# A planner that lets VectorE and GpSimd take turns and deals elementwise work to either

## The chip, the core and the metric

The kernel runs on one core of a Trainium2 chip. A core has five engines, each with its own queue of instructions that it works off in order: TensorE (PE, matrix products), VectorE (DVE), ScalarE (ACT), GpSimd (POOL) and SyncE (SP, which here issues the transfers). The metric is the device time of one execution in microseconds (us). Three runs of the kernel before gave 2014.33, 2015.26 and 2022.29 us; the median is 2015.26 us.

## What is computed

One layer of a hybrid decoder on 16 meta tokens and 1024 tokens of 1024 features, all in float32. The part that the change touches is the mixer's input:

```python
h = xn @ w_in                      # xn: (1040, 1024), w_in: (1024, 8192)
b_c, c_c, h_c, q, k, v, g_conv, g_attn = jnp.split(h, list(splits), axis=-1)
y_conv = b_c * causal_dwconv(c_c * h_c, conv_w_mix)
o = stick_breaking_attention(q.reshape(hd), k.reshape(hd), v.reshape(hd))
gate_conv = jax.nn.sigmoid(g_conv + b_gate[0])
gate_attn = jax.nn.sigmoid(g_attn + b_gate[1])
merged = gate_conv * (y_conv @ w_proj_conv) + gate_attn * (o @ w_proj_attn)
return merged @ w_out
```

Attention weighs the earlier position s for the position t by sigmoid(z_ts) times the product of (1 - sigmoid(z_tj)) over the j between s and t; the kernel makes that product with a scan. A gated MLP with a depthwise convolution follows, with norms around both parts.

## The kernel before

**Products in two halves.** Each float32 operand is split into a high half, rounded by a ScalarE copy into a narrower float type, and a lower half, the rest, from a subtraction. A product is three matmuls: high by high, high by lower, lower by high. The 8192 columns of `w_in` are 64 blocks of 128. Tokens lie along the free dimension: 1040, of which the outputs mostly use 1026 (`NQ`, from `T0` = 14), in three chunks of 342 (`CH`; for k and v the first chunk has 356).

**Plain and Strassen blocks.** A *plain* block (`plain`) is 8 k-steps by 3 chunks by 3 matmuls, 72 in all. It needs its raw weights (tag `raw`, 2 buffers), their halves (`whi` and `wlo`, 2 buffers each), and a PSUM bank. Two blocks together can be made as a *Strassen pair* (`strassen_pair`): seven products in place of eight, each of two parts of 12 matmuls with 260 columns, 168 in all. A pair needs seven weight operands, made from quarters of the two raw tiles by four sums (`dve`, lines 743 and 162) and seven splits (`keep`: ScalarE line 731, lower half line 429). They live in four `ap` buffers and in the `wlo` and `whi` buffers. It also needs the token tiles T1 to T4 (`tops`), which are sums and differences of halves of the normalised tokens: for each of four quarters `kb` two sums of 1040 columns (lines 612 and 617), then four differences of 520 and four splits, in a chain from T1 to T4.

**Stages.** First the tokens are normalised and turned into `xnT`, with two thirds of the blocks v0 and q0 between. Then comes the first plan: the last third of v0 and q0, three plain blocks (k0, v1, q1), 22 Strassen pairs and one plain gate block as a bridge. What follows a block is added to the plan too: `done_qk` splits q and k and stores them; `done_v` takes differences, transposes them (line 569) and splits them; `done_ch` and `done_b` make the convolution; `done_gate` or `gate_out` the sigmoid. The second plan is attention: per pair of heads two heads, each in three groups, with scores (958 and 959), a sigmoid on ScalarE (964), the scan on VectorE (975), transposes (994), the split into `ah` (ScalarE, 999) and `al` (VectorE, 429), the weighing matmuls (1009 and 1010), and on GpSimd the add of two parts (1039) and a last add (1052). Twelve gate blocks (`mid_gates`) are plain blocks mixed in between. The code behind is not planned in this way.

**The planner.** `Plan.run` lays the tasks out on a clock of its own while the program is built. A task has an engine, a cost, the tasks it comes after, a due key, and the slots that it takes and frees (`raw`, `whi`, `wk` and so on). Whenever an engine is free on that clock, the ready task with the lowest key whose slots are free is issued to it. So the plan sets the order of each engine's queue; on the chip, waits on semaphores keep what depends on what. An engine's task counts as done for other engines after its `LAG`. The costs are straight lines in the number of columns (`act_cost`, `dve_cost`, `pool_cost`). Each task names one engine: sums on VectorE, lower halves of weights on GpSimd, lower halves of the token tiles on either by name (T1 and T3 GpSimd, T2 and T4 VectorE). VectorE and GpSimd don't know of each other. A task's loads come at its key less 16 (plain) or less 30 (pair).

Of the kernel before, what the change touches and what calls it, by code (L numbers as in the profile page):

```python
# [17 lines left out]
P = 128  # L18
# [17 lines left out]
class Plan:  # L36
    LAG = {"PE": 0.22, "ACT": 0.1, "DVE": 0.1, "POOL": 0.1, "SP": 3.5, None: 0.0}

    def __init__(self, slots):
        self.slots = dict(slots)  # L40
        self.tasks = []

    def add(self, engine, cost, emit, after=(), key=0.0, takes=(), frees=()):
        t = SimpleNamespace(engine=engine, cost=cost, emit=emit, key=key, takes=takes, frees=frees,
                            users=[], left=0, number=len(self.tasks))
# [10 lines left out]
    def run(self):  # L56
# [4 lines left out]
        def enter(t):  # L61
            insort(ready[t.engine], (t.key, t.number, t))
# [4 lines left out]
        while done < len(self.tasks):  # L67
            moved = True
            while moved:
                moved = False  # L70
                for e in Plan.LAG:
                    if e is not None and free[e] > now + 1e-9:
                        continue
                    for i, (_, _, t) in enumerate(ready[e]):
                        if all(self.slots[k] >= t.takes.count(k) for k in t.takes):
                            break
# [3 lines left out]
                    for k in t.takes:  # L80
                        self.slots[k] -= 1
                    if t.emit is not None:
# [8 lines left out]
            while events and events[0][0] <= now + 1e-9:  # L91
                _, _, near, t = heappop(events)
                if not near:
# [28 lines left out]
def block_kernel(ctx, tc, x, meta_tokens, g_pre_mix, w_in, channels, w_proj_conv,  # L122
# [215 lines left out]
    strassen_gate, bridge_gate = gates[0], gates[1]  # L338
# [13 lines left out]
    def lo_piece(raw, hi, lo, i):  # L352
        c = slice(256 * i, 256 * i + 256)
        nc.gpsimd.tensor_tensor(lo[:, c], raw[:, c], hi[:, c].bitcast(F32), op=ALU.subtract)
# [72 lines left out]

    def low(eng, out, src, hi):
        eng.tensor_tensor(out, src, hi.bitcast(F32), op=ALU.subtract)  # L429

    def plain(o, chunks, key, make, evac, finish, psum, first_chunk=0, given=None):
        st = {}
        if given is None:
# [3 lines left out]
            def high():  # L437
# [12 lines left out]
        for ci in range(first_chunk, 3):  # L450
# [36 lines left out]
    def done_ch(cb, key):  # L487
# [4 lines left out]
        def product():  # L492
            nc.gpsimd.tensor_tensor(c(), c(), y(), op=ALU.mult)
# [9 lines left out]
        t = plan.add("POOL", pool_cost(NT), product, tuple(after1) + tuple(after2), key + 2)  # L503
        t = plan.add("ACT", act_cost(NQ), scaled, (t,), key + 5)
        t = plan.add("DVE", dve_cost(NQ), lambda: added(1), (t,), key + 7)
        t = plan.add("DVE", dve_cost(NQ), lambda: added(0), (t,), key + 8)
# [3 lines left out]
    def done_b(cb, u, after, key):  # L510
        y, after2 = mixed.pop(("y", cb))

        def product():
            nc.vector.tensor_tensor(y()[:, :NQ], y()[:, :NQ], u()[:, T0:], op=ALU.mult)

        t = plan.add("DVE", dve_cost(NQ), product, tuple(after) + tuple(after2), key + 4)
# [3 lines left out]

    def done_gate(which):
        def done(ob, u, after, key):
            t = plan.add("ACT", act_cost(NQ), lambda: nc.scalar.activation(
                u()[:, T0:], u()[:, T0:], AF.Sigmoid, bias=bias_gate(which, ob)), tuple(after), key + 3)
            plan.add("SP", 0.4, lambda: nc.sync.dma_start(
                (gc_d, ga_d)[which][ob * P:(ob + 1) * P, :], u()[:, T0:]), (t,), key + 4, (), ("wk",))
        return done

    def done_qk(hi_d, lo_d, t0):
        def done(p, u, after, key):  # L530
# [6 lines left out]
            def lower():  # L537
                low(nc.vector, u().bitcast(F32R)[:, t0:], u()[:, t0:], st["hi"])

            h = plan.add("ACT", act_cost(n), high, tuple(after), key + 3, ("wk",))  # L540
            t = plan.add("DVE", dve_cost(n), lower, (h,), key + 4)
# [6 lines left out]
    def done_v(p, u, after, key):  # L548
        st = {}

        def diff():
            st["dv"] = wk_tile("dv")
            nc.vector.tensor_tensor(st["dv"][:, 1:], u()[:, :NT - 1], u()[:, 1:], op=ALU.subtract)
# [1226 lines left out]
```

## Time and profile before

| | us |
|---|---|
| median of three runs | 2015.26 |
| the profiled execution | 2014.96 |
| its span | 2012.9 |
| TensorE busy | 1921.6 |
| VectorE busy | 1089.6 |
| ScalarE busy | 842.1 |
| GpSimd busy | 907.7 |

The span is the time from the first to the last recorded instruction. Busy time is the time in which an engine had an instruction running; matmuls are pipelined, so neighbouring ones overlap in the records, and a matmul's rate is read from the distance of starts. On VectorE, ScalarE and GpSimd neighbours overlap a little too. The granted clock of TensorE is 1.00 at full speed. In a row of the waits stand the waiting instruction, what released it, the time in total, how often, and the longest. In a row of the timeline stand start, duration, engine, line and operation, with the idle time before it in brackets. Line 429 is a helper (`low`) and line 162 another (`sub`): such rows are told apart by their tiles.

### The profile page before, as it was taken

Reading aid. Unit: us, or ns where it says so; the run is one execution under the profiler, and the core shown is the slowest. Engines: PE = TensorE matmul, PEld = TensorE weight load, DVE = VectorE, ACT = ScalarE, POOL = GpSimd, SP = SyncE. Lnnn points to the kernel's source line nnn. Section 1 sums busy time; section 2 is a strip of 40 time slices with the busy share of each in tenths; the row PEclk is TensorE's granted clock in tenths of the full one; section 3 lists DMA queues with packets and bytes.
Section 4 is the critical chain, followed back from the end, with each engine's and each line's share of the span. In section 5 each row is a group of like instructions: output and inputs, shape, how many; then the busy total and the mean of one; then the engine's idle time right before and its main releaser. Section 6 shows DMA issues by size and latency. Waiting matters only on the chain.

```text
span 2012.9 us, 32307 instructions
## 1 busy us (share of the span) xinstructions
PE 1921.6 (95%) x12756; PEld 1806.6 (90%) x12756; DVE 1089.6 (54%) x1585; ACT 842.1 (42%) x1774; POOL 907.7 (45%) x676
## 2 busy tenths in 40 slices
PE   6699999999999999999999999979999999999997
PEld 6699999999998999989899999968988998888886
DVE  6835554454438787787541126874354445345547
ACT  4433333343446666666531224453443344321122
POOL 2745665544432324242223650355556565654353
PEclk9899999999999999999999999989999999999999
DMA  3222122445587454542484673213122212253223
GB/s 138 97 88 83 64 65 63 135 144 152 167 212 169 129 136 130 137 129 60 126 250 155 185 216 115 94 33 124 63 84 71 98 66 82 89 175 113 84 84 136
DMA packets 73843, 238.56 MB, mean 119 GB/s; under 512 B 15400, under 2 KB 17224, under 8 KB 72668
## 3 DMA queue, kind: packets, MB, share of 16 engines
q1 hardware_dynamic: 70368, 226.00, 37.3%
q10 hardware_dynamic: 3324, 10.50, 1.6%
q8 instruction: 100, 1.64, 0.3%
q14 instruction: 51, 0.42, 0.1%
HBM read 166.02 MB, written 70.46 MB: 117 GB/s over the span
## 4 chain that ended last, share of the span: by engine, by line
PE 73%; DVE 12%; ACT 3%; POOL 3%; DMA 2%; issue 2%; ACTq 0%; DVEq 0%; SPq 0%; POOLq 0%
PE st L1396 7%; PE st L1398 7%; PE st L1400 7%; PE st L776 7%; PE st L779 7%; PE st L778 7%; DVE fl L975 4%; PE st L1690 3%; PE st L1688 3%; PE st L1689 3%; PE mm L231 2%; PE tp L994 2%; PE mm L233 2%; PE mm L232 2%; PE mm L331 2%
## 5 line engine op out<-in xcount | busy, mean ns | idle before, releaser
L429 POOL TENSOR_TENSOR s_op<-raw,s_op 128x512 fp32r<-128x512 f32 x132 | 184.3, 1399 | 153.3 <-ACT s_op L731 150.6
L159 POOL TENSOR_TENSOR a_op<-raw,a_op 128x512 fp32r<-128x512 f32 (+1 forms) x136 | 194.5, 1444 | 88.6 <-ACT a_op L158 84.4
L975 DVE TENSOR_TENSOR_SCAN fl<-fl,upper 114x128 f32<-114x128 f32 (+3 forms) x144 | 207.4, 1451 | 48.4 <-ACT fl L964 47.9
L776 PE MATMUL st<-tT,s_op 128*128 128x260 f32 x704 | 201.5, 286 | 12.7 <-ACT tT L638 8.1
L778 PE MATMUL st<-tT,s_op 128*128 128x260 f32 x704 | 199.9, 284 | 0.8 <-POOL tT L429 0.8
L779 PE MATMUL st<-tT,s_op 128*128 128x260 f32 x704 | 199.6, 284 | 0.0
L1396 PE MATMUL st<-opT,a_op 128*128 128x258 f32 (+2 forms) x528 | 171.2, 324 | 3.8 <-ACT snap L1411 2.3
L162 DVE TENSOR_TENSOR raw<-raw 128x512 f32<-128x512 f32 x88 | 95.6, 1086 | 141.8 <-POOL a_op L159 106.8
L1398 PE MATMUL st<-opT,a_op 128*128 128x258 f32 (+2 forms) x528 | 169.4, 321 | 2.1 <-DVE opT L159 1.1
L1400 PE MATMUL st<-opT,a_op 128*128 128x258 f32 (+2 forms) x528 | 169.2, 320 | 0.0
L1039 POOL TENSOR_TENSOR ot<-ot,half 64x342 f32<-64x342 f32 x48 | 63.3, 1318 | 211.1 <-ACT ot L1035 199.8
L158 ACT CAST a_op<-raw 128x512 fp32r<-128x512 f32 (+1 forms) x136 | 85.1, 634 | 157.5 <-DMA raw<-in_w_up_gate_dram 53.8
L731 ACT CAST s_op<-raw 128x512 fp32r<-128x512 f32 x132 | 82.1, 623 | 161.9 <-PE st L779 100.8
L776 PE MATMUL st<-xnT,s_op 128*128 128x260 f32 x528 | 149.2, 283 | 0.0
L779 PE MATMUL st<-xnT,s_op 128*128 128x260 f32 x528 | 149.0, 282 | 0.0
L778 PE MATMUL st<-xnT,s_op 128*128 128x260 f32 x528 | 148.6, 281 | 0.0
L1695 DVE TENSOR_TENSOR acc<-acc,st 128x512 f32<-128x512 f32 x144 | 98.5, 687 | 91.1 <-PE st L1690 91.1
L429 DVE TENSOR_TENSOR al<-tp,ah 114x342 fp32r<-114x342 f32 (+3 forms) x288 | 117.8, 440 | 53.5 <-ACT ah L999 52.4
L776 PEld LDWEIGHTS st<-tT,s_op 128*128 128x128 f32 x704 | 133.0, 189 | 14.1 <-ACT tT L638 8.3
L999 ACT CAST ah<-tp 114x342 fp32r<-114x342 f32 (+3 forms) x288 | 108.0, 401 | 73.7 <-PE tp L994 69.0
L778 PEld LDWEIGHTS st<-tT,s_op 128*128 128x128 f32 x704 | 133.1, 189 | 1.1 <-POOL tT L429 1.1
L779 PEld LDWEIGHTS st<-tT,s_op 128*128 128x128 f32 x704 | 133.5, 190 | 0.0
(216 smaller groups left out, 5963.8 us busy)
## 6 DMA issues: line engine op xcount, KB each, us to landing
raw<-in_w_in_dram SPq DMA_DIRECT2D x64, 512.0 KB
raw<-in_w_up_gate_dram SPq DMA_DIRECT2D x44, 512.0 KB
act_d<-owork SPq DMA_DIRECT2D x22, 512.0 KB
araw<-act_d SPq DMA_DIRECT2D x22, 512.0 KB
raw<-in_w_down_dram SPq DMA_DIRECT2D x22, 512.0 KB
qh<-qh_d SPq DMA_DIRECT2D x32, 256.5 KB
ql<-ql_d SPq DMA_DIRECT2D x32, 256.5 KB
vv_d<-vt SPq DMA_DIRECT2D x16, 512.0 KB
```

The lines of the kernel that those rows point to most:

```text
L159: (lo_engine or nc.vector).tensor_tensor(lo, src, hi.bitcast(F32), op=ALU.subtract)
L162: engine.tensor_tensor(out, a, b, op=ALU.subtract)
L429: eng.tensor_tensor(out, src, hi.bitcast(F32), op=ALU.subtract)
L776: nc.tensor.matmul(ps, wt[:, 0, c], xh, start=start and kb == 0, stop=False, skip_group_check=True)
L778: nc.tensor.matmul(ps, wt[:, 0, c], xl, start=False, stop=False, skip_group_check=True)
L779: nc.tensor.matmul(ps, wt[:, 1, c], xh, start=False, stop=kb == 3, skip_group_check=True)
L975: nc.vector.tensor_tensor_scan(fl[:, ::-1], fl[:, ::-1], upper[:, NT - nk:][:, ::-1], 1.0, op0=ALU.mult, op1=ALU.max)
L999: nc.scalar.copy(kst["ah"][:n, off:], kst["tp"][:n, off:CH])
L1396: nc.tensor.matmul(ps, wt[:, 0, k], xh, start=start and kb == 0, stop=False, skip_group_check=True)
L1398: nc.tensor.matmul(ps, wt[:, 0, k], xl, start=False, stop=False, skip_group_check=True)
L1400: nc.tensor.matmul(ps, wt[:, 1, k], xh, start=False, stop=stop and kb == 3, skip_group_check=True)
L1695: nc.vector.tensor_tensor(a, a, ps, op=ALU.add)
```

## The change

The planner gets a slot `port`, of which there is one. A task with `port` set takes it when issued and gives it back at its end; tasks of GpSimd have it, tasks of the new kind `ANY`, and on VectorE the scans and the two multiply-adds of the convolution. `ANY` tasks stand in the lists of both VectorE and GpSimd; whichever is free first on the plan's clock takes the task, and VectorE is asked first. Dealt like this are now: the token tiles' sums, differences and lower halves; the weights' sums and lower halves of the pairs; the lower halves of plain weights, in 2 pieces of 512 in place of 4 of 256, the second due 3 later; the lower halves of q and k; the differences of v; the products of the convolution; in attention the adds of lines 1039 and 1052. The cost lines and lags are changed. The first plan has two more plain blocks, k1 and the first gate, ahead of the pairs, and 21 pairs; the other blocks move up in their pairs. The token tiles' due keys are spread from 10 to 14 per quarter and from 2 to 3 per tile.

```diff
-    LAG = {"PE": 0.22, "ACT": 0.1, "DVE": 0.1, "POOL": 0.1, "SP": 3.5, None: 0.0}
+    LAG = {"PE": 0.22, "ACT": 0.18, "DVE": 0.13, "POOL": 0.13, "SP": 3.5, None: 0.0}
...
-        self.slots = dict(slots)
+        self.slots = dict(slots, port=1)
...
+                            frees=frees, port=port or engine in ("POOL", "ANY"), users=[], left=0, number=len(self.tasks))
...
-            insort(ready[t.engine], (t.key, t.number, t))
+            for e in ("DVE", "POOL") if t.engine == "ANY" else (t.engine,):
+                insort(ready[e], (t.key, t.number, t))
...
-                        if all(self.slots[k] >= t.takes.count(k) for k in t.takes):
+                        if (not t.port or self.slots["port"]) and all(
+                                self.slots[k] >= t.takes.count(k) for k in t.takes):
...
+                    if t.engine == "ANY":
+                        other = ready["POOL" if e == "DVE" else "DVE"]
+                        del other[[r[2] for r in other].index(t)]
+                        t.engine, t.cost = e, t.cost[e]
+                        t.emit(e)
...
+                if near:
+                    self.slots["port"] += t.port
...
 def act_cost(n):
-    return 0.15 + 0.00089 * n
+    return 0.045 + 0.00091 * n
 def dve_cost(n):
-    return 0.10 + 0.00117 * n
+    return 0.07 + 0.00104 * n
 def pool_cost(n):
-    return 0.12 + 0.0024 * n
+    return 0.06 + 0.0023 * n
+def any_cost(n):
+    return {"DVE": dve_cost(n), "POOL": pool_cost(n)}
...
-            los = [plan.add("POOL", pool_cost(256),
-                            lambda i=i: lo_piece(st["raw"], st["hi"], st["lo"], i), (h,), key - 9)
-                   for i in range(4)]
+            los = [plan.add("ANY", any_cost(512),
+                            lambda e, i=i: lo_piece(st["raw"], st["hi"], st["lo"], i, e, 512), (h,),
+                            key - 9 + 3 * i) for i in range(2)]
...
-                                  (before, los[kb // 2] if los else None), at,
+                                  (before, los[kb // 4] if los else None), at,
...
-        key = 10.0 * kb
-        ta = plan.add("DVE", dve_cost(NT), tile_a, (), key, ("wk", "xw"))
-        tb = plan.add("POOL", pool_cost(NT), tile_b, (), key, ("wk",))
+        key, t_step = 14.0 * kb, 3.0
+        ta = plan.add("ANY", any_cost(NT), tile_a, (), key, ("wk", "xw"))
+        tb = plan.add("ANY", any_cost(NT), tile_b, (), key, ("wk",))
...
-            k2 = key + 2 * j + 1
+            k2 = key + t_step * (j + 1)
...
-    for name in (("k", 0), ("v", 1), ("q", 1)):
+    for name in (("k", 0), ("v", 1), ("q", 1), ("k", 1)):
         o, k, done = block[name]
         plain(o, CH_K, at, *plain_out(done, k, 0), bank)
         at += item
+    which, ob = early_gate
+    plain(48 + 8 * which + ob, CH_Q, at, *gate_out(which, ob, lambda: wk_tile("gt"), ("wk",)), bank)
+    at += item
...
-    order += [("k", 1), ("v", 2), ("q", 2), ("k", 2), ("v", 3), ("q", 3), ("k", 3), ("v", 4),
-              ("q", 4), ("k", 4), ("v", 5), ("q", 5), ("k", 5), ("v", 6), ("q", 6), ("k", 6),
-              ("v", 7), ("q", 7), ("k", 7)]
+    order += [(x, k) for k in range(2, 8) for x in "vqk"]
...
-                    scans[b] = plan.add("DVE", 0.12 + 0.00225 * nk, scan, tuple(sigs), t_b + 1)
+                    scans[b] = plan.add("DVE", dve_cost(2 * nk), scan, tuple(sigs), t_b + 1, port=True)
...
-                    last_av = plan.add("PE", 2 * pe_cost(m) + 0.06, weigh, (hh, ll, v_ld, last_av), t_k + 1,
+                    last_av = plan.add("PE", 2 * pe_cost(m) + 0.08, weigh, (hh, ll, v_ld, last_av), t_k + 1,
...
-                ot_parts.append(plan.add("POOL", pool_cost(CH), out3, (o1, o2), t_o, (), ("half",)))
+                ot_parts.append(plan.add("ANY", any_cost(CH), out3, (o1, o2), t_o, (), ("half",)))
...
-        fin = plan.add("POOL", pool_cost(NQ), last_add, tuple(ot_parts), t_o + 1)
+        fin = plan.add("ANY", any_cost(NQ), last_add, tuple(ot_parts), t_o + 1)
```

More of the change, by code (lines that the diff above doesn't have):

```diff
@@ L511, in done_b, with product @@
         y, after2 = mixed.pop(("y", cb))
-        def product():
-            nc.vector.tensor_tensor(y()[:, :NQ], y()[:, :NQ], u()[:, T0:], op=ALU.mult)
-        t = plan.add("DVE", dve_cost(NQ), product, tuple(after) + tuple(after2), key + 4)
+        def product(e):
+            engine_of(e).tensor_tensor(y()[:, :NQ], y()[:, :NQ], u()[:, T0:], op=ALU.mult)
+        t = plan.add("ANY", any_cost(NQ), product, tuple(after) + tuple(after2), key + 4)
         plan.join((t,), ("wk",))
@@ L519, in done_b @@
                  (t,), key + 5, (), ("wk",))
[L521 to L527, printed above, removed]
     def done_qk(hi_d, lo_d, t0):
@@ L535, in high, with lower @@
                 nc.scalar.copy(st["hi"], u()[:, t0:])
-            def lower():
-                low(nc.vector, u().bitcast(F32R)[:, t0:], u()[:, t0:], st["hi"])
+            def lower(e):
+                low(engine_of(e), u().bitcast(F32R)[:, t0:], u()[:, t0:], st["hi"])
             h = plan.add("ACT", act_cost(n), high, tuple(after), key + 3, ("wk",))
-            t = plan.add("DVE", dve_cost(n), lower, (h,), key + 4)
+            t = plan.add("ANY", any_cost(n), lower, (h,), key + 4)
             s1 = plan.add("SP", 0.4, lambda: nc.sync.dma_start(hi_d[rows, :], st["hi"].bitcast(F32)), (h,), key + 4)
@@ L559, in done_v @@
                      tuple(after), key + 3)
-        d = plan.add("DVE", dve_cost(NT), diff, tuple(after), key + 3, ("wk",))
+        d = plan.add("ANY", any_cost(NT), diff, tuple(after), key + 3, ("wk",))
         f = plan.add("ACT", 0.2, edge, (d,), key + 4)
@@ L654, in late_tile, with gate_out, make, evac @@
         return lambda: u["t"]
+    def gate_out(which, ob, tile_of, space):
+        u = {}
+        def make():
+            u["t"] = tile_of()
+        def evac(a, n, ps):
+            nc.scalar.activation(u["t"][:, a - T0:a - T0 + n], ps, AF.Sigmoid, bias=bias_gate(which, ob))
+        def finish(after, key):
+            plan.add("SP", 0.4, lambda: nc.sync.dma_start(
+                (gc_d, ga_d)[which][ob * P:(ob + 1) * P, :], u["t"][:, :NQ]), tuple(after), key, (), space)
+        return make, evac, finish
     def plain_out(done, k, t0):
@@ L845, in block_kernel @@
         at += 14 * prod
-    def gate_out(which, ob, tile_of, space):
-        u = {}
-        def make():
-            u["t"] = tile_of()
-        def evac(a, n, ps):
-            nc.scalar.activation(u["t"][:, a - T0:a - T0 + n], ps, AF.Sigmoid, bias=bias_gate(which, ob))
-        def finish(after, key):
-            plan.add("SP", 0.4, lambda: nc.sync.dma_start(
-                (gc_d, ga_d)[which][ob * P:(ob + 1) * P, :], u["t"][:, :NQ]), tuple(after), key, (), space)
-        return make, evac, finish
     which, ob = bridge_gate
@@ L875, in block_kernel @@
     h = plan.add("ACT", act_cost(D), next_high, (ld,), at - 10, ("whi", "wlo"))
-    plan.join([plan.add("POOL", pool_cost(256), lambda j=j: lo_piece(nxt["raw"], nxt["hi"], nxt["lo"], j),
-                        (h,), at - 9) for j in range(4)], ("raw",))
+    plan.join([plan.add("ANY", any_cost(512),
+                        lambda e, j=j: lo_piece(nxt["raw"], nxt["hi"], nxt["lo"], j, e, 512),
+                        (h,), at - 9) for j in range(2)], ("raw",))
     plan.run()
```

86 lines of the change are left out of this document (42 added, 44 removed).

## The prediction

> **What bounds the kernel now.** I read the page's head first, then the table of stretches, then TensorE's waits, then single instructions on VectorE and GpSimd.
>
> ```profile
> span 2012.9 us, 32307 instructions
> PE 1921.6 (95%) x12756; PEld 1806.6 (90%) x12756; DVE 1089.6 (54%) x1585; ACT 842.1 (42%) x1774; POOL 907.7 (45%) x676
> ```
>
> TensorE (PE) sets the time: it is idle for 91 us of the span, and that is all that another order of the same work can win. The profiled execution took 2014.96 us, so 2.1 us lie outside the span; the median of the three runs is 2015.26, the same to 0.02%. I sum against 2014.96.
>
> Where the 91 us lie, by stretches (columns: length, then busy time and instruction count of PE, PEld, DVE, ACT, POOL, then the granted clock, the DMA share and GB/s):
>
> ```profile
> 44.30:52.30 8.00, 7.95 (x48) 7.60 (x48) 7.94 (x6) 0.34 (x4) 6.75 (x2) 1.00 0.01 2
> 52.30:62.40 10.10, 5.15 (x21) 4.78 (x21) 8.57 (x8) 6.18 (x10) 9.42 (x8) 0.66 0.02 4
> 62.40:87.60 25.20, 25.20 (x168) 25.06 (x166) 19.32 (x17) 9.99 (x19) 21.14 (x15) 1.00 0.43 143
> 87.60:106.60 19.00, 5.35 (x23) 4.69 (x23) 12.87 (x13) 6.33 (x14) 9.16 (x7) 0.64 0.25 92
> 106.60:595.00 488.40, 483.88 (x3952) 482.42 (x3950) 225.95 (x287) 191.11 (x394) 246.34 (x180) 1.00 0.39 116
> 595.00:991.00 396.00, 376.24 (x2609) 357.62 (x2608) 305.90 (x428) 259.78 (x666) 127.22 (x104) 1.00 0.47 125
> ```
>
> The first planner lays out everything from 44 to about 595 us, the second one attention, about 595 to 991. PE has two holes early in the first plan, is nearly full from 106.6 to 595 (4.5 us idle), and loses 19.8 us in attention. The rest (before 44 us, after 991 us) belongs to code that the change does not touch. What each hole waits for:
>
> ```profile
> PE st L776 <- ACT tT L638: 8.1, 1, 8.1
> PE st L569 <- DVE dv L553: 4.7, 1, 4.7
> PE st L776 <- ACT snap_e L786: 4.5, 6, 0.9
> PE st L331 <- ACT whi L439: 2.5, 1, 2.5
> PE st L333 <- POOL wlo L354: 2.5, 1, 2.5
> PE av L1010 <- DVE al L429: 11.4, 20, 1.8
> PE tp L994 <- DVE al L429: 6.0, 6, 1.3
> ```
>
> Hole A (52.3 to 62.4) is the first whole plain block, k0, waiting for its weights' two halves; hole B (87.6 to 106.6) is the first Strassen pair waiting for the token tiles T1 to T4. After each wait the granted clock is low too (0.66 and 0.64 above), so I price a hole by the work done in it. A plain block runs two chunks of 342 columns between the first two of these rows, and its chunk of 356 between the second and third:
>
> ```profile
> 64.49 0.32 PE L331 MATMUL st<-xnT,whi 128*128 128x342 f32 x1
> 72.06 0.33 PE L331 MATMUL st<-xnT,whi 128*128 128x356 f32 x1
> 75.97 0.32 PE L331 MATMUL st<-xnT,whi 128*128 128x342 f32 x1
> 450.00:500.00 50.00, 50.00 (x420) 50.00 (x419) 23.78 (x36) 21.04 (x45) 23.64 (x18) 1.00 0.52 153
> 106.00:595.00 489.00, 6.87 (x54) 6.05 (x54) 1.00 0.39 116
> ```
>
> So 48 matmuls of 342 columns take 7.57 us (0.158 each), 24 of 356 take 3.91 (0.163), a Strassen matmul 50/420 = 0.119, and a transpose of line 569 6.87/54 = 0.127 (last row: that line alone). Hole A did 12 wide matmuls and 9 transposes, 3.1 us of work in 10.1: lost 7.0. Hole B did 9 transposes and 14 Strassen matmuls, 2.8 in 19.0: lost 16.2. Together 23.2 us.
>
> Why the operands are late: VectorE and GpSimd slow each other, which the planner of before does not count.
>
> ```profile
> 56.08 5.17 POOL L354 TENSOR_TENSOR wlo<-raw,whi 128x256 fp32r<-128x256 f32 x4
> 119.84 2.81 POOL L354 TENSOR_TENSOR wlo<-raw,whi 128x256 fp32r<-128x256 f32 x4 [8.88 <-issue]
> 57.14 1.22 DVE L162 TENSOR_TENSOR xa<-xa 128x520 f32<-128x520 f32 x1
> 94.40 0.69 DVE L162 TENSOR_TENSOR xa<-xa 128x520 f32<-128x520 f32 x1
> 76.98 2.32 DVE L612 TENSOR_TENSOR xa<-xnT 128x1040 f32<-128x1040 f32 x1
> 92.64 1.23 DVE L612 TENSOR_TENSOR xa<-xnT 128x1040 f32<-128x1040 f32 x1
> 93.79 0.69 DVE L429 TENSOR_TENSOR tT<-xb,tT 128x520 fp32r<-128x520 f32 x1
> 95.82 1.28 POOL L429 TENSOR_TENSOR tT<-xa,tT 128x520 fp32r<-128x520 f32 x1 [4.81 <-ACT tT L638]
> 213.54 2.44 POOL L493 TENSOR_TENSOR su<-su 128x1040 f32<-128x1040 f32 x1 [1.46 <-DVE su L800]
> ```
>
> The same four GpSimd pieces take 5.17 us beside VectorE work and 2.81 alone; a VectorE subtraction 1.22 beside them and 0.69 alone. Each waits its turn: side by side, a pair costs the sum of both. The Trainium skill ("SBUF — State Buffer", Who interferes with whom) says the same as a rule, an exclusive lock held for the whole instruction, taken by GpSimd and by VectorE operations with two SBUF inputs; the rows agree.
>
> **The change, part by part.** The new cost lines and lags cost nothing themselves; they change the order in which each queue gets its work, and with the parts below decide what waits.
>
> *Dealing the token tiles.* Alone, and started one behind the other, VectorE takes 0.61 for 520 columns (from 93.79 to 94.40) and 1.15 for 1040 (92.64 to 93.79), GpSimd 1.28 and 2.44. Per quarter, before: VectorE 1 sum of 1040 and 6 of 520, GpSimd 1 of 1040 and 2 of 520: 4 × (1.15 + 3.66 + 2.44 + 2.56) = 39.2 us of turns. After: the planner looks at VectorE first, and a free turn nearly always finds it free, so I take most of it there: 4 × (2.3 + 8 × 0.61) = 28.7 us. The upper bound is the 39.2 of before.
>
> *The two blocks moved ahead.* k1 (3.91 + 7.57) and a gate block (3 × 3.785) cost 22.8 us; the pair removed costs 168 × 0.119 = 20.0. This is +2.8 us of PE work with no cover, as PE is full after 106.6. In return PE has work while the tiles are made. By the due keys, the first pair's loads come at key − 30 and the gate block's at − 27, and there are two raw buffers, so I expect only k0, v1, q1, k1 ahead of the pair and the gate inside it, as q1 lies inside it now (its weights are the 119.84 row). PE is then fed from 52.3 for 4 × 11.48 + 18 transposes (2.3) + the first product (24 × 0.119 = 2.9) = 51.1 us, to 103.4, when it first needs T1. Turns needed by then, from 44.7: tiles 28.7; weights of four blocks 8 × 0.61 = 4.9; two differences of v and three lower halves of q and k 5 × 1.15 = 5.8; four sums and four lower halves of the pair 4.9: 44.3 us, done at 89. That leaves 14 us. With all tiles at the old 39.2 it is 99.5, still in time. Hole B goes: −16.2. What comes next on PE is Strassen work with its operands ready. The loads of k1 and the gate stand in for the pair's two, 512 KB each, and move past v2's and q2's in SP's queue; the gate's store comes some 440 us earlier. The DMA share there is 0.43 and 0.25 (rows above), so they cost nothing; where a load came late, PE would wait for it as in hole A.
>
> *Hole A.* The two weight buffers come free when PE ends v0's last chunk, half way through the 44.3 to 52.3 row; then a ScalarE cast (1.05 in the row below) and a lower piece (0.61) are needed. Before, the cast stood on ScalarE behind two token tile casts, which waited for VectorE sums that took twice their time; the pieces stood behind two tile operations on GpSimd.
>
> ```profile
> 53.70 1.05 ACT L439 CAST whi<-raw 128x1024 fp32r<-128x1024 f32 x1
> 52.27 1.18 ACT L638 CAST tT<-xa 128x520 fp32r<-128x520 f32 x2 [7.62 <-DVE xa L162]
> ```
>
> With the taking of turns in the plan, the cast should start near 48.7 and the first piece end by 51.5. −7.0 if so, 0 if the queues stay as they are. I leave 2.0 us of A and B together for drift between plan and chip: −21.2 for both.
>
> *Strassen stage.* 4.5 us idle, all behind one ScalarE queue: a snapshot copy behind a scaling that waits for GpSimd's 2.44 us product. VectorE does it in 1.15. Bounds: −4.5, and +2 if dealing makes new waits of that kind. I take −2.0. The wider pieces (512, first k-step waits for half instead of a quarter) cost nothing while weights are made a block ahead, which the two buffers allow; uncovered, each block would wait 0.6.
>
> *Attention.* Dealt here: 48 adds, 8 last adds, 22 weight pieces. What they meet:
>
> ```profile
> 702.21 1.90 POOL L1052 TENSOR_TENSOR ot<-ot,ends 128x1026 f32<-128x1026 f32 x1
> 702.76 3.53 DVE L975 TENSOR_TENSOR_SCAN fl<-fl,upper 114x1040 f32<-114x1040 f32 x1 [0.34 <-ACT fl L964]
> 730.65 2.31 DVE L975 TENSOR_TENSOR_SCAN fl<-fl,upper 114x1040 f32<-114x1040 f32 x1
> L975 DVE TENSOR_TENSOR_SCAN fl<-fl,upper 114x1040 f32<-114x1040 f32 x16 | 42.8, 2677 | 1.2 <-ACT fl L964 1.2
> L1039 POOL TENSOR_TENSOR ot<-ot,half 64x342 f32<-64x342 f32 x48 | 63.3, 1318 | 211.1 <-ACT ot L1035 199.8
> ```
>
> A scan beside GpSimd took 3.53 instead of 2.31; over the 16 longest the mean excess is 0.37, so 5.9 us, perhaps 10 with the shorter ones. PE's 17.4 us of waits for al are partly this: al queues behind such a scan. A plan that knows the turns should avoid some; but VectorE, 306 of 396 us busy, gets work that GpSimd had. Bounds: −15 (nearly all waits) to +10 (the present waits half as long again). Nearest is the scans' own excess, half of it on PE's path: −3.0.
>
> The sum: −21.2 + 2.8 − 2.0 − 3.0 = −23.4, so 2014.96 − 23.4 = 1991.6 us.
>
> **The rivals.**
>
> *The hole only moves (0.10).* The tiles' due keys are spread too: the last goes from 37 to 54, 17 us later, and PE gets 22.8 us more. If the tiles come at their keys and hole A stays, only 22.8 − 17 = 5.8 us is won, less 2.8: 2012. Against it: a key is an order, not a start, and the turns are free by 89.
>
> *Attention clears as well (0.12).* Its waits fall by 15 and the Strassen stage's by 3: 2014.96 − 21.2 + 2.8 − 18 = 1978.5. For it: 17.4 of the 19.8 us are waits for al. Against it: VectorE is 77% busy.
>
> *VectorE becomes the bound in attention (0.06).* If all is dealt to VectorE: 48 adds at about 0.43 (0.61 × 342/520 and a fixed part), 8 at 1.15, 22 at 0.61, or 43 us, taking it from 306 to some 340 of 396 with the scans freed of their excess. If each stands ahead of an al on which PE waits, with no gate matmul to fill: 2014.96 − 20.4 + 43 = 2037.6. It is slower from 20.4 of the 43 us uncovered. Against it: twelve gate blocks fill PE, and al has four buffers.
>
> *The longer hold (0.04).* A GpSimd weight piece of 512 keeps its turn for about 1.28 (the 520 row), not 0.70 (2.81/4). If all 22 go to GpSimd and each holds up a scan on PE's path, 22 × 0.58 = 12.8 is given back: 2014.96 − 20.4 + 12.8 = 2007.4. The lock rule cited above is what speaks for it: by that rule nothing gives way within an instruction, as the 3.53 row shows.
>
> That the change does not do what it says, the turns being kept in the plan while the chip's queues drift together again, is the first rival's outcome by another road and is in its 0.10.
>
> **How the numbers follow.** Forecast 0.68, at 1991.6; its own range 1984 to 2002 comes from its bounds (early residue 0 to 9, Strassen −4.5 to +2, attention −6 to +4, not all at one end). To hold 8 in 10 I add the cleared attention below and the longer hold above: 1977 to 2008, which leaves out 0.16. About 0.5% (10 us) is what a measurement of this kernel can tell from no change: faster by more 0.68 + 0.12 = 0.80; within it 0.10 + 0.04 = 0.14; slower 0.06.
>
> **What would show it.** Hole A: PE's wait for whi and wlo near 52 us gone, the granted clock at 1.00 from 52 to 64. Hole B: no wait on tT over 2 us; T4's last lower half before 95 us. Dealing: most tile sums on VectorE at 0.69 and 1.23, GpSimd's busy time in the first 100 us under half of 50. Swap: 144 more plain and 168 fewer Strassen matmuls. Strassen: under 3 us idle. Attention: al waits between 8 and 20 us, long scans near 2.31. I am wrong if PE has a new hole over 5 us between 52 and 120, or if attention is over 10 us longer.

## The result, and the profile after

The changed kernel took 2030.09 us, the median of five runs (2029.43 to 2034.75), against 2015.26 of the kernel before (five runs, 2014.03 to 2022.29). The ratio is 1.0075, with a 95% interval of 1.0053 to 1.0097. It is slower, where 23 us less had been forecast. The profiled execution took 2030.09 us, so it stands for the median. Its page begins:

```profile
span 2028.3 us, 32023 instructions
PE 1931.6 (95%) x12732; PEld 1811.0 (89%) x12732; DVE 1161.1 (57%) x1784; ACT 842.6 (42%) x1766; POOL 580.1 (29%) x432
```

PE has 24 instructions fewer (144 plain more, 168 Strassen fewer, as the blocks say), and yet it is busy 10 us longer. GpSimd lost a third of its busy time, to VectorE. To find the place I cut both executions at three events that both have: the start of the first plan's feed (44.3 us), the first score matmul, and the last weighing of attention. Before, in the table of stretches (columns as in the prediction), with 250 us of the Strassen stage as the fourth row:

```profile
44.30:585.70 541.40, 518.23 (x4144) 515.45 (x4145) 268.88 (x322) 208.57 (x427) 292.28 (x208) 0.98 0.36 110
585.70:981.20 395.50, 375.74 (x2608) 356.94 (x2607) 310.83 (x432) 261.82 (x669) 124.92 (x102) 1.00 0.49 128
981.20:2012.90 1031.70, 999.32 (x5840) 907.78 (x5839) 481.80 (x760) 347.02 (x627) 483.26 (x352) 0.99 0.37 118
150.00:400.00 250.00, 245.48 (x2035) 244.22 (x2034) 125.80 (x150) 93.17 (x195) 143.82 (x93) 1.00 0.25 80
```

The same of the changed kernel, with the first stretch after 52 us:

```profile
44.30:558.00 513.70, 513.70 (x4120) 513.40 (x4120) 308.91 (x469) 208.25 (x418) 46.21 (x36) 1.00 0.39 115
558.00:998.30 440.30, 393.37 (x2612) 365.84 (x2611) 339.11 (x482) 262.61 (x669) 47.76 (x32) 0.97 0.46 116
998.30:2028.30 1030.00, 996.29 (x5837) 905.48 (x5835) 484.94 (x762) 347.13 (x627) 478.94 (x350) 0.99 0.37 118
150.00:400.00 250.00, 250.00 (x2087) 250.00 (x2086) 159.01 (x238) 97.95 (x202) 15.78 (x13) 1.00 0.26 84
52.00:64.00 12.00, 12.00 (x80) 11.97 (x79) 9.83 (x17) 7.33 (x14) 5.50 (x3) 1.00 0.54 185
```

Length by length: the first plan went from 541.4 to 513.7 (−27.7), attention from 395.5 to 440.3 (+44.8), the rest from 1031.7 to 1030.0 (−1.7). The sum is +15.4, the difference of the two spans. So the change did in its first plan what was forecast, and more; the loss is all in attention. There PE has the same work (2612 instructions against 2608), but it is idle for 46.9 us (440.30 − 393.37) instead of 19.8, and busy for 17.6 us more at a mean granted clock of 0.97. What PE waits for in attention after (waiting instruction, releaser, us in total, times, longest):

```profile
PE av L1017 <- DVE al L447: 37.5, 32, 2.6
PE z L966 <- DMA ql<-ql_d: 4.1, 1, 4.1
PE tp L1001 <- DVE al L447: 2.9, 4, 0.7
```

The weighing matmuls wait for `al`, the lower half that VectorE makes: 40.4 us in both rows, against 17.4 before. One such place, all engines in order of time (start, duration, engine, line, operation; idle time before it and its end in brackets):

```profile
695.56 3.89 DVE L982 TENSOR_TENSOR_SCAN fl<-fl,upper 114x470 f32<-114x470 f32 x3
...
695.90 0.84 PE L1001 MATMUL tp<-ident,fl 114*114 114x114 f32 x7
696.20 1.08 ACT L1006 CAST ah<-tp 114x114 fp32r<-114x114 f32 x3 [0.83 <-PE tp L1001]
...
697.54 0.22 PE L1016 MATMUL av<-ah,vv 114*128 114x114 f32 x1
699.37 1.08 DVE L447 TENSOR_TENSOR al<-tp,ah 114x114 fp32r<-114x114 f32 x3
...
699.67 0.32 PE L1017 MATMUL av<-al,vv 114*128 114x114 f32 x1 [1.91 <-DVE al L447]
```

The first cast ends some 0.26 us after 696.20 (a 114-column cast takes 0.26, in a row below), so `al` could start near 696.5. VectorE is in a run of three scans until 699.4. PE has six gate matmuls to do meanwhile, which last it until 697.5. What then happens to its clock, in three neighbouring stretches of 3.41 us:

```profile
696.83:700.24 3.41, 1.50 (x12) 1.31 (x11) 3.41 (x5) 1.20 (x4) 0.00 (x0) 1.00 0.57 182
700.24:703.65 3.41, 3.41 (x16) 3.36 (x15) 2.08 (x5) 1.79 (x5) 0.00 (x0) 0.50 0.00 1
703.65:707.07 3.42, 3.42 (x26) 3.34 (x25) 1.32 (x3) 1.53 (x4) 0.00 (x0) 1.00 0.01 2
```

A wait of 1.91 us, the idle part of the first row, is followed by 3.41 us at half clock, in which 1.7 us of full-speed work are lost. In the changed kernel's attention the clock is at half in six places, 23.9 us in all, so 12 us of full-speed work are lost, 3.4 of them behind the wait for ql at its start. Before, it was one place of 3.4 us, 1.7 lost. So the +44.8 reads as 27.2 us of idle time and 17.6 of slower and sparser matmuls, some 10 of which are the clock. That is a reading; no run changes the one and keeps the other.

I also laid PE's idle stretches in attention over what VectorE was running in them, instruction by instruction:

```
us of PE's idle time    in all   VectorE in a scan   in an al   in an add
before                    19.8         9.2              8.9        0.0
changed                   46.9        25.0             13.3        3.6
```

More than half of the new idle time is time in which VectorE was in a scan; 40.4 of the 46.9 us in all end with an `al`.

### The profile page after: what moved, and what is told of

Its sections match the earlier page's. It is cut to its first block, busy times and chain, and to the rows that moved or that the text cites. A ratio compares the mean times of both kernels' runs of the same rounds, so it can differ in the third digit from the quotient of the medians.

```text
span 2028.3 us, 32023 instructions
## 1 busy us (share of the span) xinstructions
PE 1931.6 (95%) x12732; PEld 1811.0 (89%) x12732; DVE 1161.1 (57%) x1784; ACT 842.6 (42%) x1766; POOL 580.1 (29%) x432
## 4 chain that ended last, share of the span: by engine, by line
PE 74%; DVE 13%; DMA 5%; ACT 3%; POOL 2%; issue 2%; SPq 0%; ACTq 0%; DVEq 0%; POOLq 0%
PE st L796 7%; PE st L799 7%; PE st L798 7%; PE st L1403 6%; PE st L1407 6%; PE st L1405 6%; DVE fl L982 5%; PE st L1697 3%; PE st L1695 3%; PE st L1696 3%; PE mm L245 2%; PE tp L1001 2%; PE mm L246 2%; PE mm L247 2%; DVE al L447 2%
## 5 line engine op out<-in xcount | busy, mean ns | idle before, releaser
L796 PE MATMUL st<-tT,s_op 128*128 128x260 f32 x672 | 190.9, 284 | 0.0
L799 PE MATMUL st<-tT,s_op 128*128 128x260 f32 x672 | 190.1, 283 | 0.0
L798 PE MATMUL st<-tT,s_op 128*128 128x260 f32 x672 | 190.0, 283 | 0.0
L796 PE MATMUL st<-xnT,s_op 128*128 128x260 f32 x504 | 142.4, 283 | 0.0
L799 PE MATMUL st<-xnT,s_op 128*128 128x260 f32 x504 | 142.3, 282 | 0.0
L798 PE MATMUL st<-xnT,s_op 128*128 128x260 f32 x504 | 141.8, 281 | 0.0
L176 DVE TENSOR_TENSOR raw<-raw 128x512 f32<-128x512 f32 x72 | 73.8, 1026 | 108.1 <-POOL a_op L173 106.3
L447 DVE TENSOR_TENSOR s_op<-raw,s_op 128x512 fp32r<-128x512 f32 x121 | 84.4, 698 | 78.8 <-ACT s_op L751 78.3
L1017 PE MATMUL av<-al,vv 114*128 114x342 f32 (+3 forms) x288 | 92.1, 332 | 38.3 <-DVE al L447 37.5
L1405 PE MATMUL st<-opB,a_op 128*128 128x512 f32 (+2 forms) x396 | 127.4, 322 | 0.0
L1403 PE MATMUL st<-opB,a_op 128*128 128x512 f32 (+2 forms) x396 | 127.4, 322 | 0.0
L1407 PE MATMUL st<-opB,a_op 128*128 128x512 f32 (+2 forms) x396 | 126.9, 321 | 0.0
```

Source lines behind the costliest of these rows:

```text
L796: nc.tensor.matmul(ps, wt[:, 0, c], xh, start=start and kb == 0, stop=False, skip_group_check=True)
L798: nc.tensor.matmul(ps, wt[:, 0, c], xl, start=False, stop=False, skip_group_check=True)
L799: nc.tensor.matmul(ps, wt[:, 1, c], xh, start=False, stop=kb == 3, skip_group_check=True)
L1017: nc.tensor.matmul(av[:, off:], w, kst["al"][:n, off:], start=False, stop=(kb == nkb - 1))
L1403: nc.tensor.matmul(ps, wt[:, 0, k], xh, start=start and kb == 0, stop=False, skip_group_check=True)
L1405: nc.tensor.matmul(ps, wt[:, 0, k], xl, start=False, stop=False, skip_group_check=True)
```

## The experiments

All but one are the changed kernel with an edit; all compute the whole layer. Where an edit concerns the cost lines, they are set anew where the plan of attention starts, and the first plan keeps the changed ones. The measures are the time of the first score matmul (when the first plan is over), the length of attention from there to the last weighing, and the total. The kernel before, on the same chips, had medians of 2015.01 to 2017.80 us. Single executions of one attention plan differ by some 3 us (shown below), so I read nothing into less.

### The first four: is it attention's plan, and which part of it

Four parts of the change reach attention: the adds dealt to VectorE, the wider weight pieces, the turns (`port`), and the cost lines with the lags. First, all of them undone together, in attention alone.

```diff
-    plan = Plan({"raw": 2, ...})
+    Plan.LAG = {"PE": 0.22, "ACT": 0.1, "DVE": 0.1, "POOL": 0.1, "SP": 3.5, None: 0.0}
+    COST.update(act=(0.15, 0.00089), dve=(0.10, 0.00117), pool=(0.12, 0.0024))
+    plan = Plan({"raw": 2, ..., "port": 99})
```

With these lines go the adds on POOL by name, weight pieces of 256 on POOL, and the scans' and weighings' own costs, all as before.

> The changed first plan with the attention plan of before (its costs, lags, engines, weight pieces, no port). The loss lies in the attention plan: from the first score matmul to the last weighing matmul 395.7 us before, 440.4 changed; the first plan ends 27.7 us earlier. If the attention plan itself is the cause, attention here takes 396 to 404 (404 if the wait for the loads at its start stays) and the total is 1988 to 1997. Rival: attention is slow because of what the first plan leaves behind (the loads late, the clock low after the hole, data in other buffers): then attention stays over 420 and the total over 2010.

```profile
557.50:954.60 397.10, 376.13 (x2609) 357.17 (x2607) 311.00 (x432) 261.37 (x669) 124.70 (x102) 1.00 0.49 128
```

Attention is back at 397.1, with the clock at 1.00. The median is 1992.71 us, 0.9877 of before (0.9858 to 0.9897). So the first plan's gain is real and stays, and all of the loss lies in how attention is planned.

Then each part. The 48 adds and 8 last adds back on GpSimd:

```diff
-ot_parts.append(plan.add("ANY", any_cost(CH), out3, ...))
+ot_parts.append(plan.add("POOL", pool_cost(CH), lambda f=out3: f("POOL"), ...))
...
-fin = plan.add("ANY", any_cost(NQ), last_add, ...)
+fin = plan.add("POOL", pool_cost(NQ), lambda f=last_add: f("POOL"), ...)
```

> The changed kernel, with the 48 adds and 8 last adds of attention on GpSimd by name as before, everything else changed. Theory A (the adds dealt to VectorE stand ahead of al, the third rival of the prediction): attention falls from 440 to under 410, PE's waits for al from 40 us to under 20. Theory B (tighter costs and lags make a plan that the chip cannot keep) and theory C (the port slot reorders the scans): attention stays at 430 or more.

```profile
558.50:995.80 437.30, 400.13 (x2613) 372.61 (x2612) 323.84 (x436) 263.00 (x669) 111.12 (x78) 0.95 0.46 116
```

VectorE is 15 us less busy, and attention hardly shorter (437.3; total 2030.40). That was the rival by which VectorE becomes the bound through dealt work; without the adds, which were most of it, the loss stays. The 22 weight pieces are still dealt here. They are in the next run too, with all else that is dealt: the cost lines and lags of before alone, everything else as changed:

```diff
+    Plan.LAG = {"PE": 0.22, "ACT": 0.1, "DVE": 0.1, "POOL": 0.1, "SP": 3.5, None: 0.0}
+    COST.update(act=(0.15, 0.00089), dve=(0.10, 0.00117), pool=(0.12, 0.0024))
```

> The changed kernel, with the cost lines and lags of before in the attention plan alone. Theory B: attention falls to under 410, since old ScalarE costs (0.45 us for 342 columns against 0.36) put slack between ah, al and the weighing. Theories A and C: it stays at 430 or more.

```profile
557.50:962.30 404.80, 377.65 (x2609) 359.20 (x2608) 331.49 (x474) 262.97 (x669) 53.37 (x40) 1.00 0.50 126
```

404.8, and 1994.78 in all: the lines and lags carry nearly all of the loss, although VectorE is busy for 331 us, 20 more than with the whole plan of before. So the rival of the dealt work falls as a whole; the wider pieces were not undone by themselves, and at most the 7.7 us from 397.1 to 404.8 are left for them and the rest. Last the turns, switched off in attention by 99 ports:

> The changed kernel, with as many port slots as wanted in the attention plan, so that VectorE and GpSimd do not take turns there; the dealing and the costs stay. Theory C: attention falls to under 415. Theories A and B: it stays within 10 us of 440.

Attention 430.7, total 2026.60: 10 us of the 45.

### Lines or lags, and which line

The two parts of that edit by themselves, and then one line at a time.

```diff
# lines of before, lags as changed
+    COST.update(act=(0.15, 0.00089), dve=(0.10, 0.00117), pool=(0.12, 0.0024))
# lags of before, lines as changed
+    Plan.LAG = {"PE": 0.22, "ACT": 0.1, "DVE": 0.1, "POOL": 0.1, "SP": 3.5, None: 0.0}
# ScalarE's line alone as before
+    COST.update(act=(0.15, 0.00089))
# VectorE's line alone as before
+    COST.update(dve=(0.10, 0.00117))
```

> The changed kernel, with the cost lines of before in the attention plan and the new lags. If the cost lines hurt, attention is 400 to 410 and the total 1990 to 1998. If the lags do, it stays at 430 or more.

> The changed kernel, with the lags of before (ScalarE, VectorE and GpSimd 0.1) in the attention plan and the new cost lines. If the lags are what hurt, attention falls from 440 us towards the 405 that old costs and lags together gave. If the cost lines hurt, it stays at 430 or more; shorter lags let the plan weigh even sooner, so over 440 is possible.

> The changed kernel, with ScalarE's cost line alone as before in the attention plan (0.454 us in place of 0.356 for 342 columns). If slack on ScalarE is what the chip needs (it feeds both scan and al), attention falls to under 415. If VectorE's line is what matters, it stays over 425.

> The changed kernel, with VectorE's cost line alone as before in the attention plan (scan of 1040 at 2.53 us by the double length in place of 2.23, al of 342 at 0.50 in place of 0.43). If slack on VectorE is what the chip needs, attention falls to under 415. If ScalarE's line is what matters, it stays over 425. If both runs with one line land half way, slack as such is what counts.

| | attention | total |
|---|---|---|
| changed | 440.3 | 2030.09 |
| lines of before, lags as changed | 400.0 | 1990.19 |
| lags of before, lines as changed | 435.5 | 2025.97 |
| ScalarE's line of before | 411.7 | 1999.36 |
| VectorE's line of before | 418.8 | 2010.51 |

It is the lines. One alone brings back 28.6 or 21.5 of the 44.8, together more than the 40.3 of both, so they overlap: to plan one of the two steps between transposes and weighing longer already helps. For VectorE's line I had written down under 415 and over 425; it landed between.

### What in the lines: the fixed part

How do the lines stand to the records? Of the changed kernel's attention, groups by line and form (count, busy us, mean ns of one, idle us before it and its ends). ScalarE first, then VectorE:

```profile
L1006 ACT CAST ah<-tp 114x342 fp32r<-114x342 f32 x144 | 61.1, 450 | 52.6 <-PE tp L1001 49.6 <-PE av L1016 2.3
...
L1006 ACT CAST ah<-tp 114x114 fp32r<-114x114 f32 x48 | 12.6, 263 | 23.0 <-PE tp L1001 22.9
```

```profile
L447 DVE TENSOR_TENSOR al<-tp,ah 114x342 fp32r<-114x342 f32 x144 | 69.2, 501 | 30.0 <-ACT ah L1006 29.4
...
L982 DVE TENSOR_TENSOR_SCAN fl<-fl,upper 114x1040 f32<-114x1040 f32 x16 | 37.1, 2318 | 3.6 <-ACT fl L971 3.6
...
L447 DVE TENSOR_TENSOR al<-tp,ah 114x114 fp32r<-114x114 f32 x48 | 12.5, 260 | 8.3 <-ACT ah L1006 8.1
```

A cast of 114 columns takes 0.263 us. The old line says 0.15 + 0.00089 × 114 = 0.251, the new one 0.045 + 0.00091 × 114 = 0.149. With 342 columns it is 0.450, 0.454 and 0.356. `al` with 342 takes 0.501: old 0.500, new 0.426. So the old lines are close to the recorded durations; the new ones leave out about 0.1 us of each ScalarE instruction, which is what two back-to-back instructions overlap (two casts of 342 columns that follow each other at 700.82 take 0.78 together, not 0.90). As a statement of throughput the new line is no worse; as a statement of when a lone cast is done it is short, and many casts here are lone: the 192 in these two rows had 75.6 us of idle time before them, ended nearly always by a transpose. The Trainium skill ("ScalarE: Activation LUTs", What ACT_TABLE_LOAD costs) states 186 ns plus 0.833 ns a column for an ACTIVATE with immediate scale and bias, and an overlap of about 93 ns for ACTIVATEs back to back. Taken over to these casts, that is an estimate of 281 ns for 114 columns, and 263 were measured. The lags of the changed kernel (0.18 in place of 0.1) give the 0.1 back to whoever waits, but not to ScalarE's own calendar. To test the fixed part by itself, it alone is put back and the new slopes stay:

```diff
+    COST.update(act=(0.15, 0.00091), dve=(0.10, 0.00104), pool=(0.06, 0.0023))
```

> The changed kernel with only the fixed parts of two lines as before in the attention plan: ScalarE 0.15 in place of 0.045, VectorE 0.10 in place of 0.07, all slopes new. If what hurt is that short operations were planned far too short (0.15 us for a ScalarE cast of 114 columns that takes 0.26), nearly all comes back: attention 398 to 406. If the slopes matter (VectorE's scans at 2.23 for 1040 columns in place of 2.53), it stays at 408 to 420, as with ScalarE's line alone (411.7).

```profile
558.20:957.90 399.70, 380.04 (x2611) 358.10 (x2609) 334.42 (x478) 263.12 (x669) 51.16 (x36) 1.00 0.51 127
```

Its waits in attention:

```profile
PE av L1023 <- DVE al L452: 12.3, 22, 1.5
PE z L972 <- DMA ql<-ql_d: 2.5, 1, 2.5
PE tp L1007 <- DVE al L452: 2.1, 2, 1.1
```

399.7 and 1990.12 us: 0.105 us on each ScalarE task and 0.03 on each VectorE task of the plan are worth 40 us. The waits for `al` fall from 40.4 to 14.4, none over 1.5 us, and the clock is back at 1.00.

If short is bad, is long better? Two steps up, the first of them run by itself and then timed, and the turns off on top of the old lines:

```diff
# pad: more than recorded
+    COST.update(act=(0.25, 0.00089), dve=(0.15, 0.00117), pool=(0.12, 0.0024))
# pad further
+    COST.update(act=(0.35, 0.00089), dve=(0.25, 0.00117), pool=(0.12, 0.0024))
# lines of before, 99 ports in attention
+    COST.update(act=(0.15, 0.00089), dve=(0.10, 0.00117), pool=(0.12, 0.0024))
```

> The changed kernel with still longer cost lines in the attention plan: ScalarE 0.25 + 0.00089 n and VectorE 0.15 + 0.00117 n, 0.1 and 0.05 over the lines of before. If slack as such is what the chip wants, attention falls below the 400.0 us that the lines of before gave. If a line should be as long as the recorded duration (0.16 + 0.00085 n on ScalarE) and no longer, attention is 403 to 425, as the plan's own clock grows with it.

> The kernel of the run with longer lines again (ScalarE 0.25 + 0.00089 n, VectorE 0.15 + 0.00117 n in the attention plan), now timed. In one look it took 1986.9 us with attention at 395.9. If that holds, the median is 1985 to 1991 and it is the fastest version; if the look was lucky, it is 1991 to 1995, as the lines of before gave.

> Still longer lines in the attention plan: ScalarE 0.35 + 0.00089 n, VectorE 0.25 + 0.00117 n. The plan then holds ScalarE busy for 433 us and VectorE for 429, more than PE's 386, so the order is laid out as if they were the bound. If slack goes on helping, attention is under 396. If the order suffers once PE is no longer the bound on the plan's clock, it is 405 or more.

> The old cost lines in the attention plan and no turns there (as many port slots as wanted). With the new lines, taking the turns away won 10 us (440.3 to 430.7). If the turns themselves order the scans badly, attention falls here too, from 400.0 to 390 to 396. If they only hurt on top of lines that are too short, it is 398 to 406.

| | attention | total |
|---|---|---|
| pad, single execution | 395.9 | 1986.94 |
| pad, timed | 399.0 | 1991.80 (median; 1990.17 to 1998.25) |
| pad further | 408.5 | 2005.66 |
| lines of before, turns off | 402.5 | 1990.66 |

The pad seemed the best version by its single execution; timed, at a ratio of 0.9884 (0.9863 to 0.9904), it is no better than the lines of before. Under 400 was written down for it in case slack as such is what the chip wants, and 403 to 425 in case a line should be no longer than the record. The second did not come, and the first can't be told from 400.0. Lines that are 0.1 us too long on ScalarE and 0.05 on VectorE cost nothing that shows, where 0.105 and 0.03 too short cost 40. Too long by 0.2 and 0.15 costs some 9. Turns on or off make no difference once the lines are right, so the 10 us above were theirs only on top of the short lines.

Could the one order of the changed kernel be bad by accident? Four different plans with both lines short took 430.7 to 440.3, the two with one short line 411.7 and 418.8, and five with both fixed parts as before or 0.1 and 0.05 longer 395.9 to 404.8. So it goes with the lines and not with one order.

### The first plan: blocks, planner, and the wait for ql

The kernel before, with only the new order of blocks (k1 and the first gate ahead, 21 pairs) and its own planner:

```diff
-    for name in (("k", 0), ("v", 1), ("q", 1)):
+    for name in (("k", 0), ("v", 1), ("q", 1), ("k", 1)):
...
+    which, ob = strassen_gate
+    plain(48 + 8 * which + ob, CH_Q, at, *gate_out(which, ob, lambda: wk_tile("gt"), ("wk",)), bank)
```

> The kernel before, its planner and costs untouched, with the new order of blocks alone: k1 and the gate ahead, 21 pairs. From PE's first planned matmul at 44 us to the first score matmul it took 541.4 us before and 513.7 with the whole change. If the blocks alone cover the tiles, it is 515 to 525 here; if it is the planner's taking of turns that makes the operands ready, both holes stay at about 7 and over 5 us and it is 527 to 541. Attention's plan is the old one: 395 to 402.

Its waits up to 575 us:

```profile
PE st L569 <- DVE dv L553: 9.0, 1, 9.0
PE st L789 <- ACT snap_e L799: 4.4, 6, 0.9
PE st L331 <- ACT whi L439: 2.5, 1, 2.5
PE st L333 <- POOL wlo L354: 2.5, 1, 2.5
```

The first plan takes 538.6 us from 44.3, 2.8 less than before; I had expected 515 to 525 if the blocks alone cover the tiles and 527 to 541 if the planner's turns are needed, and it is the second; the rows say more. The wait on `tT` is gone, as PE has work for it, and a 9.0 us wait for v's differences stands in its place; hole A is untouched. The first plan as changed took 512.5 to 514.6 us in fourteen executions, so 2.8 is hardly more than their spread. The opposite, the changed planner with the old order and 22 pairs (and the old lines in attention):

> The changed planner with the old order of blocks (three whole plain blocks, 22 pairs) and the old cost lines in attention. VectorE needed until 85 us for the tiles' lower halves where PE with two blocks less wants T1 near 80: if the blocks are needed as cover, PE has a wait on the tiles of 3 to 10 us between 75 and 100, and the first plan takes 514 to 521 us, less 2.8 for the pair that is cheaper. If the turns alone were the trouble, there is no wait and it takes 511 us, better than 513.7.

```profile
PE st L584 <- DVE dv L568: 3.7, 1, 3.7
PE mm L348 <- ACT gt L675: 1.5, 1, 1.5
```

517.9 us, with no wait for the token tiles. So of the 27.7 the planner alone brings 23.5 and the blocks alone 2.8; on top of the planner the blocks bring 4.2.

Last, an attempt to better it. In the changed order q7 and k7 make the last pair, just ahead of attention, and the first scores wait 4.1 us for ql. v2 as the early plain block, and the gate closing the last pair with k7:

```diff
-    for name in (("k", 0), ("v", 1), ("q", 1), ("k", 1)):
+    for name in (("k", 0), ("v", 1), ("q", 1), ("k", 1), ("v", 2)):
...
+    blocks.append((48 + 8 * early_gate[0] + early_gate[1], early_gate[1], done_gate))
```

> The changed kernel with the cost lines of before in the attention plan (attention 400.0 us, total 1990.2 in one look), and v2 in place of the gate among the plain blocks ahead, so that the gate closes the last pair with k7 as before. If q7 and k7 in the last pair are what holds up the first loads of attention (PE waited 2.9 to 4.1 us for ql in every run with them, not before), that wait goes and the total is 1984 to 1989, some 26 to 31 under before. If the loads are late for another reason, the wait stays and the total is 1989 to 1993.

```profile
PE mm L348 <- ACT gt L675: 1.4, 1, 1.4
PE st L584 <- DVE dv L568: 0.7, 1, 0.7
```

The wait for ql went, but the first plan took 516.3 us, so nothing was won: 1992.25, ratio 0.9876 (0.9860 to 0.9893). Half of the expectation missed. The three timed versions lie between 1991.8 and 1992.7, some 1.2% under the kernel before and 1.9% under the changed one.

## Why the prediction was right or wrong

**Hole A and hole B: right.** From 52 to 64 us PE is busy for 12.00 of 12.00 at a clock of 1.00 (the last row of the changed kernel's stretches), and over the whole first plan it is not idle at all. The steps behind it show on VectorE:

```profile
44.63 1.23 DVE L622 TENSOR_TENSOR xa<-xnT 128x1040 f32<-128x1040 f32 x1
...
46.94 0.69 DVE L176 TENSOR_TENSOR xa<-xa 128x520 f32<-128x520 f32 x1
...
51.08 1.28 DVE L369 TENSOR_TENSOR wlo<-raw,whi 128x512 fp32r<-128x512 f32 x2
...
88.43 0.69 DVE L447 TENSOR_TENSOR tT<-xb,tT 128x520 fp32r<-128x520 f32 x1
```

The sums run at 1.23 and 0.69, the durations without GpSimd beside them; of the first two weight pieces one is done near 51.7, where 51.5 was forecast, and both by 52.4; T4's last half ends at 89.1, where 89 was worked out. GpSimd was busy for 46.2 us in the first plan in place of 292.3: nearly all of the dealing went to VectorE. The 2.0 us that I left for drift were not needed. The opposite run shows that the planner made this, with the blocks as a smaller part, as "the turns are free by 89" had it. PE came to T1 later than the 103.4 us worked out, at 114.1, since the gate block ran ahead of it; so the tiles, done at 89.1, had more time than they needed. On its own clock the planner had PE without idle time in both first plans, 509.0 us before and 511.2 changed (from the built programs); the chip took 541.4 and 513.7. With the turns counted, the first plan is one that the chip keeps.

**The blocks: +2.8 in work, right within what the runs tell.** They won 2.8 to 4.2 us net, since they cover waits that the planner alone leaves (the 3.7 us for v's differences).

**Strassen: right in sign, under-sized.** I took −2.0 with −4.5 as the end, from the idle time. In 150 to 400 us the changed kernel does 2087 matmuls, the one before 2035: 52 more, 6.2 us at 0.119 each, in 4.5 us less idle time and half of the stage. Idle time of PE understates a loss where neighbouring matmuls overlap in the records.

These make −27.7 where the terms gave −21.2 + 2.8 − 2.0 = −20.4. The 2.0 of drift and 4.2 of Strassen are 6.2 of the 7.3 between.

**Attention: wrong.** The step that failed is the sentence "The new cost lines and lags cost nothing themselves; they change the order in which each queue gets its work", and with it the term of −3.0 with its bounds of −15 to +10. It was +44.8. I had priced what each operation meets (scans beside GpSimd: at 2.318 the long ones did come down from 2.677, as foreseen) and not what a plan with other numbers does to the order. Undoing the lines gives 40 of the 45 us back; undoing the dealt adds, 3. With the right lines the dealing and the turns in attention are worth nothing that shows: 399.7 to 404.8 with them, 397.1 without.

None of the four rivals was it. The third had the place and the sign, waits for al on VectorE in attention, and 2037.6 us as its price, but by the dealt work, which the runs refute; that 2030.09 lies near it is luck. The sign that I had named for being wrong, attention over 10 us longer, is the one that came.

How the short lines make al late is less settled than that they do. This is what the planner and the built queues say (no profile; the queue rows are worked out from the built program's TensorE queue at the planner's own matmul costs):

```
                                        before  changed  lines old  fixed part old
attention on the plan's own clock        397.6    399.5      402.8           401.0
measured                                 395.5    440.3      400.0           399.7
ScalarE busy by the plan                 298.7    232.7      298.7           303.2
PE work queued between the transposes
of a step and its weighing, mean of 288   2.70     2.41       2.95            2.75
steps where that is under 2 us              81      103         60              72
```

By its own clock the changed plan is as good as the others: it does not see what it loses. It believes ScalarE busy for 232.7 us where the profile has 262.6. Believing casts and al done early, it leaves less PE work between a step's transposes and its weighing (in the table, up to the matmul that reads al); on the chip the al, with a scan in front of it, takes longer than that work lasts. But the two runs with one line each have 2.71 (ScalarE's) and 2.88 (VectorE's), as good as the fast ones, and 28.9 and 32.2 us of idle time, so this count isn't the whole of it. And the built queues aren't quite the plan's: the layer that records the program puts some scans ahead of al that the plan had in front of them, in every kernel. The three scans of 695.56 are such a case; the plan had the three al first. With a scan counted once for each al that it was moved ahead of, these were 109 us of scans before, 171 in the changed kernel and 70 with the fixed part put back, but also 249 with the lines of before, which is fast. Which of the two decides stays open, and so does the split between idle time and clock: the pad, timed, had 13.7 us at half clock in attention, against 23.9, and still took 399.0.

## What to carry to other kernels

Here the planner's cost had to say when a lone instruction is done, and not only how closely a row of them can follow each other: with 0.105 us too little on ScalarE's tasks and 0.03 on VectorE's the plan was worse by 40 us on the chip and as long as ever on its own clock, while 0.1 and 0.05 us too much cost nothing that shows. So when a change retunes a cost model for one stage, measure each stage that is planned with it by itself, and give each stage its own lines if they disagree. And when a forecast counts a table of costs at nothing because it adds no instruction, it has left out the order, which here was the largest term.

## What was not expected of the hardware

A wait of 1.9 us was enough to halve TensorE's granted clock for 3.41 us (the rows from 696.83 on). A longer one, 2.51 us, left it at 1.00:

```profile
852.02 0.32 PE L1017 MATMUL av<-al,vv 114*128 114x114 f32 x1 [2.51 <-DVE al L447]
847.01:850.42 3.41, 2.50 (x17) 2.07 (x15) 3.35 (x5) 2.09 (x6) 1.90 (x1) 1.00 0.76 304
850.42:853.83 3.41, 1.81 (x14) 1.79 (x15) 2.48 (x5) 1.43 (x4) 0.00 (x0) 1.00 0.44 175
853.83:857.25 3.42, 3.42 (x26) 3.37 (x24) 2.95 (x3) 2.28 (x6) 0.00 (x0) 1.00 0.44 102
```

In all 18 traces the clock changes only at multiples of one step of 3.413 us, whose place differs from run to run. The wait of 1.91 us lay within one step; that of 2.51 was split by the border at 850.42 into 0.91 and 1.60. In the attention of the 18 traces each of the 33 full-clock steps with 1.8 us or more of PE's idle time was followed by half clock, none of the 2035 with less than 1.35, and 17 of the 54 between; ends of matmuls are modelled, so the border may be sharper than this. The Trainium skill ("TensorE: Matmul & The Clock Gate", The HAM clock gate) has an idle window of about 3.4 us for that, which runs on its own clock; the length and the fixed border agree, but here about half a window of idle time was enough. So a wait of 2 us costs more than itself when most of it falls into one step: with 40.4 us of waits for al, the longest 2.6, five of the six places at half clock lay behind one of them, and with 14.4 us, none over 1.5, none did.
